# Attention's turns at every second row block of a projection, two actions in each

## The chip, the cores and the metric

The kernel runs on one core of a Trainium2 chip. A core has a matrix engine (PE, whose weight loads the profile lists apart as PEld), a vector engine (DVE), an activation engine (ACT), a general engine (POOL) and a queue that starts transfers (SP). The engines run side by side, each through its own list of instructions in order, and wait for one another by semaphores. The metric is the device time of one execution in microseconds (us).

## The reference

One layer of a hybrid decoder in float32, for 1024 rows of width 2048. The input is normalised by its rows' root mean square, multiplied by a matrix of 2048 x 6656, and the product is cut into two groups of heads:

- **stick-breaking** (16 heads of width 64): the weight of key s for query t is sigmoid(z) times the product of 1 - sigmoid(z) over the keys between them, over all earlier keys;
- **sliding window** (16 query heads on 4 key heads): a softmax over the last 128 keys, with a bias per distance and a learned extra logit per head.

Each group's result is normalised, gated with x * sigmoid(x) of a further slice of the projection, and both together go through an output matrix of 2048 x 2048. That is normalised again and added to the input.

## The kernel before

**Precision.** Each large product is made of three matrix products: both operands are split into a high part (a type that PE reads in one pass) and the rest, and high x high, high x rest and rest x high are summed in PSUM. So a weight chunk arrives by a transfer (L131), ACT makes its high part (L133), DVE the rest (L135).

**Projections.** The width 6656 is 52 column blocks of 128. The first three are done while the input arrives (to about 77 us). The other 49 follow one by one from the list `work`; `proj` runs each over four weight chunks (kg), two halves of 512 rows (h) and four blocks of 128 of the inner dimension (j): 4 x 2 x 4 = 32 steps of three matmuls 128x128 by 128x512. One such block of the inner dimension is a "row block" here. After each of the 32 steps `proj` calls `step()`. The 49 projections thus have 1568 steps.

**Attention between the steps.** Attention is cut into units, 160 for stick-breaking (8 pairs of heads, 20 units each; key `sb`) and 64 for the sliding window (4 groups, 16 units each; key `sw`). A unit has three actions on PE:

- *s1*: four score matmuls into a bank of tag "pz" (2 banks). ACT and DVE then turn scores into weights: two sigmoids, two scans and a product for `sb` (L530 to L546); bias, maximum, exponential, sum and scaling for `sw` (L614 to L629).
- *s2*: three or four 128x128 transposes of the weights into a bank of tag "pw" (2 banks), split by ACT (L561, L640) and DVE (L562, L641).
- *s3*: four matmuls with the values into the bank of tag "po" (only one bank). For `sw` each unit ends with a copy of this bank by ACT (L493) and a transfer; for `sb` one to four units share the accumulation before the copy.

A fourth kind, from the list `later`, holds deferred pieces, above all the two transposing pieces of a value block (`evac_v`, tile `vt`), which use "pw" too.

**Who comes next.** `advance()` runs at most one action. It looks, in this order, for a deferred piece that is due, an s3, an s2, an s1. "Due" goes by the planner's own clock `pe_time`, which adds up the nominal length of the matmuls written so far (0.64 for one step, 0.43 for a score or a value action, 0.33 or 0.44 for the transposes). An s2 is due 6.2 (`sb`) or 7.0 (`sw`) after its s1 was written, an s3 4.5 or 5.0 after its s2; s1 follow one another at 4.7 or 3.8, where the first two of a group may follow at once. At most three units stand between s1 and s2, at most three between s2 and s3. The order of PE's instructions is the order in which the program writes them; the other engines' lists are ordered by a scheduler under priorities.

**Deadlines.** When the values of pair p are projected, `drain` forces whatever is left of pair p - 1 (and, at the first, of the sliding window), without waiting for the due times. `background()` runs at each step as well and moves sums for the output product through POOL by the same clock.

**Output product.** From about 1504 us on, seven products of half size (a Strassen form) make the output, L907, with row scaling and residual at the end.

Of the kernel before, what the change touches and what calls it, by code (L numbers as in the profile page):

```python
# [57 lines left out]
def layer(ctx, tc, xT, x, w_first, w_blk, w_out, g_pre, g_post, g_sb, g_sw, sinks, rel, onehot, penalty, out):  # L58
# [93 lines left out]
    def advance(force=False):  # L152
        now = pe_time[0]
        while waiting and (force or waiting[0][0] <= now):
            todo.extend(waiting.pop(0)[1])
            prep()
        if later and (force or later[0][0] <= now):
            later.pop(0)[1]()
            return True
        if stage2 and (force or stage2[0][0] + stage2[0][1]["lag2"] <= now):  # L160
            u = stage2.pop(0)[1]
            u["s3"]()
            left[u["key"]] -= 1
            return True
        if stage1 and len(stage2) < 3 and (force or stage1[0][0] + stage1[0][1]["lag"] <= now):
            u = stage1.pop(0)[1]
            u["s2"]()
            stage2.append((pe_time[0], u))
            return True
        if todo and len(stage1) < todo[0]["depth"] and (force or last_start[0] + todo[0]["period"] <= now):  # L170
            u = todo.pop(0)
            if not u["ready"]:
                u["prep"]()
            last_start[0] = max(last_start[0] + u["period"], now - u["period"])
            u["s1"]()
            stage1.append((pe_time[0], u))
            prep()
            return True
        return False

    def prep():
        for u in todo[:AHEAD]:
            if not u["ready"]:
                u["ready"] = True
                u["prep"]()
# [4 lines left out]
    def background(force=False):  # L190
        for ch in chains:
            while force or pe_time[0] >= ch["at"]:
                if ch["job"] is None:
                    if not jobs:
                        break
                    ch["job"] = jobs.pop(0)(ch["buf"])
                wait = next(ch["job"], None)
                if wait is None:
                    ch["job"] = None
                else:  # L200
                    ch["at"] = pe_time[0] + wait
# [7 lines left out]
    def open_chain(buf, start):  # L209
        chains.append(dict(buf=buf.rearrange("p (a n) -> p a n", a=2), at=start, job=None))  # L210
# [38 lines left out]
    open_chain(row_sw, 112.0)  # L249
    open_chain(at.tile([P, 2 * HALF], F32, tag="bg", name="bg", bufs=1), 122.0)  # L250

    def step():
        advance()
        background()

    def drain(key):
# [195 lines left out]
    def proj(b, name, nxt=None, mid=None):  # L452
        def get(b, name, kg):
            return split_w(f"{name}_{kg}", w_blk[b, :, 4 * kg:4 * kg + 4, :])

        if not splits:
            splits.append(get(b, name, 0))
        ps = [pproj(f"p_{name}_{h}") for h in range(2)]
        for kg in range(4):
            wh, wl = splits.pop(0)  # L460
            if kg == 2 and mid is not None:
                mid()
            if kg < 3:
                splits.append(get(b, name, kg + 1))
            elif nxt is not None:
                splits.append(get(*nxt, 0))
            for h in range(2):
                for j in range(4):
                    k = 4 * kg + j
                    for i, (wt, xt) in enumerate(((wh, xh[k]), (wh, xl[k]), (wl, xh[k]))):  # L470
                        mm(ps[h], wt[:, j, :], xt[:, h * HALF:(h + 1) * HALF],
                           start=(k == 0 and i == 0), stop=(k == KT - 1 and i == 2))
                    step()
        return ps
# [535 lines left out]
```

## Time and profile before

| | us |
|---|---|
| median of 3 runs | 1807.02 |
| lowest and highest of the 3 | 1804.5 and 1808.76 |
| the profiled execution's own time | 1807.31 |
| its span from the first to the last instruction | 1805.6 |
| PE busy | 1780.6 (99%) |
| DVE busy | 1245.8 (69%) |
| ACT busy | 789.6 (44%) |
| POOL busy | 496.0 (27%) |

Busy time is the union of an engine's instructions. PE's matmuls overlap in the pipeline: a 128x512 matmul shows some 0.39 us, but the next starts about 0.23 us later. So distances between starts say what work costs on PE, and idle time before an instruction, with its releaser, says what a wait costs. The table of waits lists who waited for whom, the timeline lists instructions by start, and a table of windows gives the busy time in stretches of the span.

### The profile page before, as it was taken

How to read it: one execution, taken by the hardware profiler on the slowest of the kernel's cores; microseconds unless marked ns; L12 is line 12 of the kernel's file. 1: busy time of each engine (PE TensorE's matmuls, PEld its weight loads, DVE VectorE, ACT ScalarE, POOL GpSimd, SP SyncE). 2: the span in 40 equal slices, each digit the busy share in tenths (PEclk: the TensorE clock that was granted, in tenths of full speed). 3: DMA queues.
4: the chain of work that ended last, by engine and by line, in shares of the span. 5: the costliest groups of instructions: out<-in, count | busy, mean ns of one | idle time of the engine just before them, and what ended most of it. 6: DMA issues, size and time to landing. Idle time of an engine off the chain costs nothing. (4 is left out here: it accounts for less than half of the span.)

```text
span 1805.6 us, 27329 instructions
## 1 busy us (share of the span) xinstructions
PE 1780.6 (99%) x9046; PEld 1492.2 (83%) x9046; DVE 1245.8 (69%) x1984; ACT 789.6 (44%) x1696; POOL 496.0 (27%) x648
## 2 busy tenths in 40 slices
PE   8999999999999999999999999999999999999997
PEld 7788888888888888888888888888888887888886
DVE  7558852588567688587776787767858657746867
ACT  7335531355344444344443444434435434445433
POOL 0011121211213333133232322232313225504523
PEclk9999999999999999999999999999999999999999
DMA  7548675576747657466556564454435386634485
GB/s 230 193 138 219 199 223 148 167 210 206 224 124 199 182 164 195 142 182 184 175 163 185 153 183 129 137 169 139 151 91 140 98 258 210 198 105 129 143 250 184
DMA packets 203884, 312.48 MB, mean 173 GB/s; under 512 B 24640, under 2 KB 84192, under 8 KB 203616
## 3 DMA queue, kind: packets, MB, share of 16 engines
q1 hardware_dynamic: 201680, 307.60, 57.7%
q10 hardware_dynamic: 2064, 3.15, 0.5%
q8 instruction: 72, 1.18, 0.3%
q14 instruction: 68, 0.56, 0.1%
HBM read 219.42 MB, written 91.23 MB: 172 GB/s over the span
## 5 line engine op out<-in xcount | busy, mean ns | idle before, releaser
L543 DVE TENSOR_TENSOR_SCAN m_sb<-m_sb,m_sb,zero 128x257 f32<-128x257 f32 x192 | 157.3, 857 | 46.9 <-ACT m_sb L530 46.4
L530 ACT ACTIVATE m_sb<-z_sb 128x512 f32<-128x512 f32 x160 | 96.1, 601 | 132.1 <-PE z_sb L122 119.9
L546 DVE TENSOR_TENSOR b_sb<-b_sb,m_sb 128x512 f32<-128x512 f32 x160 | 129.0, 806 | 20.5 <-POOL b_sb L536 9.0
L540 DVE TENSOR_TENSOR_SCAN m_sb<-m_sb,mask 128x256 f32<-128x256 f32 x128 | 117.4, 953 | 35.2 <-ACT m_sb L530 34.5
L907 PE MATMUL y<-wohi,x 128*128 128x512 f32 x448 | 140.8, 390 | 0.0
L562 DVE TENSOR_TENSOR wl_sb<-wt_sb,wh_sb 128x512 fp32r<-128x512 f32 (+1 forms) x160 | 100.7, 631 | 57.7 <-ACT wh_sb L561 57.0
L561 ACT CAST wh_sb<-wt_sb 128x512 fp32r<-128x512 f32 (+1 forms) x160 | 86.9, 543 | 111.6 <-PE wt_sb L126 109.3
L907 PE MATMUL y<-wohl,x 128*128 128x512 f32 x576 | 132.8, 389 | 2.7 <-DVE wohl L773 2.7
L907 PEld LDWEIGHTS y<-wohl,x 128*128 128x128 f32 x576 | 108.0, 188 | 25.5 <-DVE wohl L773 3.1
L122 PE MATMUL p_qsb<-xh,whi_qsb 128*128 128x512 f32 x256 | 104.5, 408 | 0.0
L122 PE MATMUL p_ksb<-xh,whi_ksb 128*128 128x512 f32 x256 | 104.4, 408 | 0.0
L122 PE MATMUL p_zsw<-xh,whi_zsw 128*128 128x512 f32 x256 | 104.3, 407 | 0.0
L122 PE MATMUL p_vsb<-xh,whi_vsb 128*128 128x512 f32 x256 | 102.9, 402 | 0.0
L122 PE MATMUL p_zsb<-xh,whi_zsb 128*128 128x512 f32 x256 | 102.9, 402 | 0.0
L623 ACT ACTIVATE L_sw<-L_sw,nm_sw 128x256 f32<-128x256 f32 (+1 forms) x128 | 62.6, 490 | 91.6 <-DVE nm_sw L618 88.5
L122 PE MATMUL p_zsw<-xh,wlo_zsw 128*128 128x512 f32 x256 | 101.0, 394 | 0.0
L122 PE MATMUL p_ksb<-xh,wlo_ksb 128*128 128x512 f32 x256 | 100.9, 394 | 0.0
L122 PE MATMUL p_qsb<-xh,wlo_qsb 128*128 128x512 f32 x256 | 100.8, 394 | 0.0
L122 PE MATMUL p_ksb<-xl,whi_ksb 128*128 128x512 f32 x256 | 100.7, 394 | 0.0
L122 PE MATMUL p_zsw<-xl,whi_zsw 128*128 128x512 f32 x256 | 100.7, 393 | 0.0
L122 PE MATMUL p_vsb<-xh,wlo_vsb 128*128 128x512 f32 x256 | 100.7, 393 | 0.0
L122 PE MATMUL p_qsb<-xl,whi_qsb 128*128 128x512 f32 x256 | 100.6, 393 | 0.0
(242 smaller groups left out, 4974.3 us busy)
## 6 DMA issues: line engine op xcount, KB each, us to landing
row_sw<-in_w_out SPq DMA_DIRECT2D x80, 256.0 KB, 4.2
bg<-in_w_out SPq DMA_DIRECT2D x80, 256.0 KB, 4.5
woraw<-wsum SPq DMA_DIRECT2D x80, 256.0 KB, 3.3
kh<-kd SPq DMA_DIRECT2D x160, 64.0 KB, 3.3
kl<-kd SPq DMA_DIRECT2D x160, 64.0 KB, 3.1
wsum<-row_sw SPq DMA_DIRECT2D x40, 256.0 KB, 2.6
wsum<-bg SPq DMA_DIRECT2D x40, 256.0 KB, 3.1
q_sw<-qd SPq DMA_DIRECT2D x64, 128.0 KB, 3.6
```

The costliest lines, as they stand in the source:

```text
L122: tc.keep_in_program_order(nc.tensor.matmul(ps, a, b, start=start, stop=stop))
L530: nc.scalar.activation(m[:, :, 1:257], z, AF.Sigmoid, scale=-SCALE)
L540: nc.vector.tensor_tensor_scan(m[:, tb, 1:257], m[:, tb, 1:257], mask[:, P - P * tb:P - P * tb + 256], m[:, tb, 0:1], ALU.mult, ALU.max)
L543: nc.vector.tensor_tensor_scan(m[:, tb, :], m[:, tb, :], zero.to_broadcast([P, 257]), prev[:, tb, 256:257], ALU.mult, ALU.max)
L546: nc.vector.tensor_mul(beta, beta, m[:, :, 0:256])
L561: nc.scalar.copy(wh[:, :k], pt[:, :k])
L562: nc.vector.tensor_sub(wl[:, :k], pt[:, :k], wh[:, :k].bitcast(F32))
L623: nc.scalar.activation(L[:, hh, :n], L[:, hh, :n], AF.Exp, bias=nm[:, hh:hh + 1], accum_out=sm[:, hh:hh + 1])
L907: nc.tensor.matmul(ps, xt[:, a, tcols], w[b][:, cols], start=first and n == 0, stop=last and n == 2)
```

## The change

`step()` is called as often as before. `background()` still runs in each call. `advance()` now runs only in every second call, and there twice, so that up to two actions are written one behind the other with no projection step between them. Since a projection has 32 steps, the turns fall on the second and fourth row block of each chunk and half. Nothing else is edited: due times, limits, tiles and the matmuls themselves are the same.

```diff
+    turn = [0]
+
     def step():
-        advance()
+        turn[0] += 1
+        if turn[0] % 2 == 0:
+            advance()
+            advance()
         background()
```

## The prediction

> **What bounds the kernel now.** I read the page's table of engines first, then the time by stages, then PE's waits.
>
> ```profile
> span 1805.6 us, 27329 instructions
> ...
> PE 1780.6 (99%) x9046; PEld 1492.2 (83%) x9046; DVE 1245.8 (69%) x1984; ACT 789.6 (44%) x1696; POOL 496.0 (27%) x648
> ```
>
> The profiled execution took 1807.31 us, 1.7 around its span; the median of the three runs, 1807.02, is 0.3 below it. PE is busy in all but 25 us. The windows say where the 25 us lie (columns: stretch, its length, then busy time of PE, PEld, DVE, ACT, POOL, granted clock, DMA):
>
> ```profile
> 77.00:490.00 413.00, 407.89 (x2126) 341.07 (x2125) 267.83 (x673) 177.37 (x544) 79.69 (x63) 1.00 0.66 190
> 490.00:630.00 140.00, 140.00 (x735) 118.38 (x734) 89.21 (x126) 55.69 (x106) 36.95 (x64) 1.00 0.63 173
> 630.00:1440.00 810.00, 808.39 (x4329) 685.25 (x4328) 593.58 (x804) 359.44 (x681) 243.24 (x421) 1.00 0.53 154
> ...
> 1500.00:1806.00 306.00, 293.49 (x1309) 241.81 (x1307) 208.41 (x266) 127.08 (x257) 119.02 (x81) 0.99 0.54 172
> ```
>
> The edit acts between 77 and 1504 us. There PE idles 5.1 us in the sliding window's stretch (77 to 490) and 1.6 us in the stick-breaking stretches (490 to 1440). The 12.5 us after 1500 belong to the output product and the tail. PE's waits by name:
>
> ```profile
> PE f0a L122 <- ACT whi_f L308: 5.8, 1, 5.8
> PE y L907 <- DVE wohl L773: 2.7, 1, 2.7
> PE wt_sw L126 <- DVE L_sw L629: 2.4, 4, 1.1
> PE vt_vsw L126 <- DVE v_vsw L396: 1.9, 1, 1.9
> PE o_sb L122 <- DVE wl_sb L562: 1.6, 3, 0.9
> PE o_sw L122 <- ACT ot_sw L493: 0.7, 1, 0.7
> ```
>
> Attention's own waits are the last four, 2.4 + 1.9 + 1.6 + 0.7 = 6.6 us. That is the most that a better order of the same actions can give back in waits. The three bigger engines beside PE have spare time everywhere, so the time is PE's instructions plus its waits.
>
> **The change part by part.** *The number of actions.* 64 + 160 units of three actions and 20 deferred transposing pieces make 692 actions in 1568 steps. On the timeline no two of them stand together now; 373 times exactly one projection step lies between two, 168 times two. The new turns are 784, with room for 1568 actions, so the capacity is as before. Nothing is added to or taken from PE: the instruction count stays, and no DMA is added. What moves is (a) an action that is due at an odd step, one step later, (b) two actions that are due together, side by side, and (c) with each s1 its successors' operand loads, on SP's queue, by one step.
>
> *Side by side on PE.* The starts around the end of the first stick-breaking pair:
>
> ```profile
> 612.75 0.28 PE L122 MATMUL o_sb<-wl_sb,v_vsb 128*128 128x256 f32 x1
> 612.87 0.40 PE L122 MATMUL p_vsb<-xh,whi_vsb 128*128 128x512 f32 x1
> ...
> 613.57 0.49 PE L126 MATMUL wt_sb<-ident,b_sb 128*128 128x128 f32 x3
> ...
> 616.65 0.39 PE L122 MATMUL p_vsb<-xh,whi_vsb 128*128 128x512 f32 x1
> ...
> 618.69 0.39 PE L122 MATMUL p_vsb<-xh,whi_vsb 128*128 128x512 f32 x1
> ...
> 619.37 0.28 PE L122 MATMUL o_sb<-wh_sb,v_vsb 128*128 128x256 f32 x1
> ...
> 621.70 0.39 PE L122 MATMUL p_vsb<-xh,wlo_vsb 128*128 128x512 f32 x1
> ```
>
> A step between two actions takes 613.57 - 612.87 = 0.70 us. Far from any action three steps take 618.69 - 616.65 = 2.04, or 0.68 each. So the visit itself costs something: averaged over the timeline, the steps between two visits are 18 ns over that floor where one step lies between, 28 where two, 42 where four, 17.0 us in all. With turns two steps apart I count about 490 visits for the 692 actions: some 380 gaps at 28 ns and 110 at 42 make 15 us, **-2 us**. The bounds are 0 (the excess goes with the actions, not with the visits) and -4 (all actions in pairs, 346 gaps at 38).
>
> *The due times hold.* An s2 still waits its 6.2 or 7.0 after its s1. Its next turn after that is on average a step away instead of half a step, so operands are on average some 0.35 us more ready. For the sliding window I worked the clock through: in the steady state s1 come every four steps, and eight steps after an s1 the clock has 8 x 0.64 + 4 x 0.43 = 6.84 < 7.0, so its s2 comes at the tenth. Now 26 of 64 come at the eighth and 26 at the ninth. The 2.4 us on L_sw should mostly go: **-1.5** (bounds -2.4 and 0, the latter because DVE's chain is in order and may be late by as much). The 1.6 us on wl_sb: **-0.8** (-1.6 to +0.8). The one wait for ot_sw in the middle of a group: **-0.4** (-0.7 to 0).
>
> *Two outputs through one bank.* At the start of a group two s1 are written at once, already now. With pairs in a turn both s2 fall into one turn too, ten steps on, and by the clock both s3 into one, six steps after that. For `sw` both write the single "po" bank, with ACT's copy between them. The first such pair now:
>
> ```profile
> 127.07 0.28 PE L122 MATMUL o_sw<-wh_sw,v_vsw 128*128 128x256 f32 x1
> ...
> 127.54 0.39 PE L122 MATMUL p_qsw<-xh,whi_qsw 128*128 128x512 f32 x1
> ...
> 127.74 0.37 ACT L493 COPY ot_sw<-o_sw 128x256 f32<-128x256 f32 x1 [0.67 <-PE o_sw L122]
> ...
> 128.24 0.31 PE L122 MATMUL o_sw<-wh_sw,v_vsw 128*128 128x256 f32 x1
> ```
>
> The step at 127.54 hides the copy exactly: it is over at 128.11 and the second s3 starts at 128.24. Without that step the second could start at 127.54 and waits until about 128.2: a new wait of 0.65 us, more if ACT is in another instruction. Here ACT had idled 0.67 before; behind a 0.6 us cast it is 1.25. Four groups at 0.7: **+2.8** (bounds +2.6 and +5). Later in a group the s3 come two steps apart by my count and the copy is covered. For `sb` the pair accumulates in one bank with no copy between: 0. The pairs of s1 and s2 have two banks of their own.
>
> *Two value pieces.* The pieces of the first value block stand one step apart, with a wait behind it:
>
> ```profile
> 87.06 0.60 PE L126 MATMUL vt_vsw<-ident,u_vsw 128*128 128x128 f32 x4
> ...
> 89.64 0.42 DVE L396 TENSOR_TENSOR v_vsw<-vt_vsw,v_vsw 128x256 fp32r<-128x256 f32 x1
> 90.21 0.99 PE L126 MATMUL vt_vsw<-ident,u_vsw 128*128 128x128 f32 x4 [1.86 <-DVE v_vsw L396]
> ```
>
> The second waits for DVE's last read of the first. The lags are 9.0 and 10.0; the sixteenth step has 10.24, so both fall into one turn, the step between them goes behind both, and the wait grows by it: **+0.7**. The clock takes part here:
>
> ```profile
> 87.00:90.00 3.00, 1.36 (x8) 0.81 (x6) 2.07 (x4) 1.78 (x4) 0.58 (x1) 1.00 0.60 172
> 90.00:94.00 4.00, 3.79 (x12) 3.19 (x13) 1.52 (x4) 1.26 (x3) 1.96 (x2) 0.57 0.76 198
> ```
>
> After a stretch with PE busy 1.36 of 3 us the granted clock is 0.57 over the next 4 us, which costs 4 x 0.43 = 1.7 us and is in the time already. With a wait of 2.6 us I keep it: 0, bounds -1.7 and +1.7 (a second stretch like it).
> The Trainium skill ("TensorE: Matmul & The Clock Gate", "Why this matters for your kernels") lets the clock drop only at idle gaps beyond about 3 us; by that neither gap would cost clock, while this row shows a drop after 1.86 us, and the row decides.
>
> *Deadlines.* The last s3 of the pair stands at 619.37, and its value projection ends three steps later (621.70 is its last matmul). By the clock, the first s1 moves from step 9 to step 10 of its pair and the last s3 from 125 to 126 of 128: two steps of margin, nothing forced, **0**. If one s3 slipped a turn, it would be forced about six steps (4.2 us) after its s2, whose operands now take a median of 2.7 us: still about 0.
>
> *Weights, SP.* The rest part of a weight chunk is ready a median of 5.7 us before its first matmul, and PE has no wait on it above 0.2 us. One step (0.70) more or less in SP's order is covered. If that cover went at one chunk per projection, each step late would cost 0.70.
>
> The sum is -2 - 1.5 - 0.8 - 0.4 + 2.8 + 0.7 = -1.2, and 1807.3 - 1.2 = **1806.1 us**.
>
> **The rivals.** *Slower: the single output bank.* If the pairs of s3 don't come only at a group's start but recur, because s2 that are due at odd steps are rounded into the same turn, each pair costs 0.65 to 1.25 us on PE with nothing to cover it. Up to 32 pairs fit in 64 units: 21 to 40 us. It decides (over 3.6 us slower than before) from about eight pairs beyond my four; at twelve beyond, at 0.65, the sum is -1.2 + 7.8 = +6.6, or 1814. For it: only a step of 0.70 covers the copy now. Against it: the due times spread the s3 by four steps in the steady state, and the group is done 41 steps or more before it is needed.
>
> *Faster: the waits go.* The pairs find ACT free and the extra lag takes all the waits but the value piece's: -2.4 - 1.6 - 0.7 in waits, -4 in visits and +0.7 + 2.6 give -5.4, or 1802. For it: 0.35 us more readiness on average; against it: the 2.6 us of the bank pairs is arithmetic.
>
> *Forced actions.* The turns lag so far that each drain forces an s2 and its s3 back to back: eight drains at about 2.7 us (median from s2 to its split's end) are +22, or 1829. Against it: last s2 eleven steps, last s3 three steps before the end, and an equal capacity.
>
> **How the numbers follow.** What a measurement of this kernel tells from no change is about 0.2%, 3.6 us. Forecast (1806, no difference) 0.58; the bank 0.18 and forced actions 0.04, both slower; the waits go 0.20, faster. So faster 0.20, same 0.58, slower 0.22. The forecast's terms give 1800 with all low bounds at once (-4 - 2.4 - 1.6 - 0.7 + 2.6 + 0.7 - 1.7 = -7.1) and 1815.5 with all high ones (0.8 + 5 + 0.7 + 1.7 = +8.2); as they don't fall together, its own range is 1802 to 1811. Reaching to the other cases, the range is 1801 to 1813, which leaves out the forced case and half of the bank's.
>
> **What would show it right or wrong.** The count of PE's instructions the same; about 490 visits; waits on ot_sw by PE four times at 0.6 to 1.3 us, near the third turn after the first s2 of each `sw` group; the wait for L_sw near 1 us; vt_vsw at 2.6 us, and the clock still down after it; no two s3 of `sb` beyond a pair's end. It is wrong if PE waits for ot_sw ten times or more, if a projection's matmuls wait for weights, or if PE's starts grow by more than 0.1 us where two actions meet.

## The result, and the profile after

The changed kernel takes 1819.30 us (median of six runs, 1813.90 to 1823.34) against 1805.72 us for the kernel before (six runs, 1803.53 to 1808.76). The ratio is **1.0078, with a 95% interval of 1.0063 to 1.0094**. It is slower, by some 14 us, where the forecast was 1806 and no difference. The profiled execution took 1823.11 us, 15.8 more than the profiled one of before, and its trace is compared with that one below.

The page's head and table of engines after the change:

```profile
span 1821.4 us, 27339 instructions
...
PE 1781.3 (98%) x9046; PEld 1500.7 (82%) x9046; DVE 1255.3 (69%) x1984; ACT 793.7 (44%) x1696; POOL 499.8 (27%) x648
```

PE's instructions are as many as before and its busy time is 0.7 us more. So nearly all of the 15.8 us is idle time of PE. The windows (stretch, length, busy time of PE, PEld, DVE, ACT, POOL, granted clock, DMA share, GB/s):

```profile
77.00:490.00 413.00, 403.92 (x2122) 342.31 (x2121) 259.15 (x673) 180.04 (x543) 78.75 (x63) 1.00 0.66 190
490.00:630.00 140.00, 133.87 (x690) 113.27 (x689) 87.52 (x119) 53.29 (x100) 35.51 (x62) 0.98 0.58 159
630.00:1440.00 810.00, 804.37 (x4301) 684.42 (x4300) 607.61 (x799) 358.85 (x678) 247.15 (x418) 1.00 0.54 154
1500.00:1822.00 322.00, 308.01 (x1366) 253.59 (x1364) 214.63 (x277) 132.83 (x268) 121.32 (x84) 0.98 0.55 175
```

PE now idles 9.1 us in the first stretch (5.1 before), 6.1 in the second (0), 5.6 in the third (1.6) and 14.0 in the last (12.5). The names of its waits:

```profile
PE o_sb L122 <- DVE wl_sb L567: 8.3, 4, 5.3
...
PE o_sw L122 <- ACT ot_sw L498: 3.1, 4, 1.4
PE wt_sb L126 <- DVE b_sb L551: 2.7, 2, 1.9
PE wt_sw L126 <- DVE L_sw L634: 2.3, 6, 1.0
PE y L912 <- DVE wohl L778: 2.2, 1, 2.2
PE vt_vsw L126 <- DVE v_vsw L401: 2.2, 1, 2.2
PE y L912 <- ACT wohi L777: 1.7, 1, 1.7
PE z_sw L122 <- DMA q_sw<-qd: 1.5, 1, 1.5
PE p_qsb L122 <- DVE wlo_qsb L135: 0.6, 1, 0.6
```

The wait on wl_sb rose from 1.6 to 8.3 us and one on b_sb of 2.7 is new. Both are in the stick-breaking stretches, where the prediction had seen almost nothing to wait for.

The starts of the projections' 1568 steps on PE's timeline say where the two kernels part. At step 480, the end of the sliding window, the changed kernel is 0.5 us ahead (it was 1.2 ahead at the first step). It loses 8.3 us between steps 512 and 544, 1.7 between 576 and 608, 2.1 between 672 and 704 and 4.1 between 832 and 864. Elsewhere behind step 480 stretches of 32 steps differ by at most 0.7 us to either side. At the last step it is 14.1 us behind, and the output product adds 1.7.

**The largest place**, at 550 to 567 us. A gate of the sliding window there needs the stored attention output, `or_zsw`, which comes in two transfers on SP's queue. SP's timeline after:

```profile
550.56 0.60 SPq L414 DMA_DIRECT2D or_zsw<-od  x1
552.00 0.55 SPq L131 DMA_DIRECT2D wraw_zsw<-in_w_blk  x1
553.70 0.60 SPq L414 DMA_DIRECT2D or_zsw<-od  x1
```

and before:

```profile
548.60 1.66 SPq L409 DMA_DIRECT2D or_zsw<-od  x2
```

Before, both transfers were issued together. Now a weight load stands between them and the second is issued at 553.70. By the profile, SP's waits just before these two were ended by landings of background transfers: 0.8 us by a load of `bg` before the weight load, 1.1 us by a store of `row_sw` before the second `or_zsw`. Before, two such waits on loads of `bg` took 0.6 and 0.5 us here. The timeline of all engines after (start, us, engine; in brackets the idle time just before and what ended it):

```profile
560.81 1.28 POOL L416 TENSOR_TENSOR or_zsw<-or_zsw 128x512 f32<-128x512 f32 x1 [12.62 <-DMA or_zsw<-od]
...
562.08 0.62 POOL L541 TENSOR_SCALAR_AFFINE_SELECT b_sb<-b_sb 128x512 f32<-128x512 f32 x1
562.66 1.26 POOL L227 TENSOR_TENSOR bg<-bg 128x512 f32<-128x512 f32 x1
562.73 1.74 DVE L551 TENSOR_TENSOR b_sb<-b_sb,m_sb 128x512 f32<-128x512 f32 x1 [6.14 <-POOL b_sb L541]
...
564.18 1.42 POOL L227 TENSOR_TENSOR row_sw<-row_sw 128x512 f32<-128x512 f32 x1
564.40 1.74 DVE L135 TENSOR_TENSOR wlo_zsw<-wraw_zsw,whi_zsw 128x512 fp32r<-128x512 f32 x1
...
566.07 0.68 DVE L567 TENSOR_TENSOR wl_sb<-wt_sb,wh_sb 128x512 fp32r<-128x512 f32 x1
...
566.80 0.58 PE L122 MATMUL o_sb<-wl_sb,v_vsb 128*128 128x256 f32 x1 [5.28 <-DVE wl_sb L567]
```

It is a chain through three lists that are each in order. POOL stands 12.62 us at the sum of the two halves. Behind it in POOL's list is the masking of a diagonal unit (b_sb, L541), and DVE waits 6.14 us for that. Then two background sums (L227) run on POOL beside two products of DVE, which take 1.74 us each. Behind these two in DVE's list is wl_sb, and PE waits 5.28 us for it. The same place before:

```profile
556.07 1.45 POOL L411 TENSOR_TENSOR or_zsw<-or_zsw 128x512 f32<-128x512 f32 x1 [7.51 <-DMA or_zsw<-od]
...
557.51 0.62 POOL L536 TENSOR_SCALAR_AFFINE_SELECT b_sb<-b_sb 128x512 f32<-128x512 f32 x1
...
558.10 1.28 POOL L227 TENSOR_TENSOR bg<-bg 128x512 f32<-128x512 f32 x1
...
558.16 1.77 DVE L546 TENSOR_TENSOR b_sb<-b_sb,m_sb 128x512 f32<-128x512 f32 x1 [1.73 <-POOL b_sb L536]
```

The chain was there before, too: POOL stood 7.51 us, and DVE's product beside a background sum took 1.77 us. It ended just early enough that PE did not wait. The change did not make this chain; it made it longer than its cover.

### The profile page after: what moved, and what is told of

It reads as the page before. It is cut to its first block, busy times and chain, and to the rows that moved or that the text cites. A ratio compares the mean times of both kernels' runs of the same rounds, so it can differ in the third digit from the quotient of the medians.

```text
span 1821.4 us, 27339 instructions
## 1 busy us (share of the span) xinstructions
PE 1781.3 (98%) x9046; PEld 1500.7 (82%) x9046; DVE 1255.3 (69%) x1984; ACT 793.7 (44%) x1696; POOL 499.8 (27%) x648
## 4 chain that ended last, share of the span: by engine, by line
PE 73%; DVE 6%; DMA 6%; issue 1%; ACT 1%; POOL 1%; SPq 1%; DVEq 0%; ACTq 0%; POOLq 0%
PE y L912 12%; PE p_zsb L122 10%; PE p_ksb L122 9%; PE p_zsw L122 8%; PE p_vsb L122 8%; PE p_qsb L122 7%; PE p_qsw L122 4%; PE o_sb L122 4%; PE z_sb L122 4%; PE wt_sb L126 3%; DMA or_zsw<-od 2%; DMA xr<-in_x 1%; PE p_vsw L122 1%; DVE y L876 1%; PE o_sw L122 1%
## 5 line engine op out<-in xcount | busy, mean ns | idle before, releaser
L548 DVE TENSOR_TENSOR_SCAN m_sb<-m_sb,m_sb,zero 128x257 f32<-128x257 f32 x192 | 151.7, 828 | 42.4 <-ACT m_sb L535 42.0
L551 DVE TENSOR_TENSOR b_sb<-b_sb,m_sb 128x512 f32<-128x512 f32 x160 | 140.7, 879 | 27.5 <-POOL b_sb L541 13.4
L545 DVE TENSOR_TENSOR_SCAN m_sb<-m_sb,mask 128x256 f32<-128x256 f32 x128 | 113.7, 929 | 37.7 <-ACT m_sb L535 37.6
L912 PEld LDWEIGHTS y<-wohi,x 128*128 128x128 f32 x448 | 84.9, 190 | 20.0 <-ACT wohi L777 2.1
L122 PE MATMUL p_vsb<-xl,whi_vsb 128*128 128x512 f32 x256 | 100.7, 393 | 0.0
L541 POOL TENSOR_SCALAR_AFFINE_SELECT b_sb<-b_sb 128x512 f32<-128x512 f32 x64 | 49.1, 768 | 187.5 <-ACT b_sb L537 184.2
```

The lines of the kernel that those rows point to most:

```text
L122: tc.keep_in_program_order(nc.tensor.matmul(ps, a, b, start=start, stop=stop))
L541: nc.gpsimd.affine_select(out=beta, in_=beta, compare_op=ALU.is_gt, fill=0.0, base=0, pattern=[[-P, 2], [1, 256]], channel_multiplier=-1)
L545: nc.vector.tensor_tensor_scan(m[:, tb, 1:257], m[:, tb, 1:257], mask[:, P - P * tb:P - P * tb + 256], m[:, tb, 0:1], ALU.mult, ALU.max)
L548: nc.vector.tensor_tensor_scan(m[:, tb, :], m[:, tb, :], zero.to_broadcast([P, 257]), prev[:, tb, 256:257], ALU.mult, ALU.max)
L551: nc.vector.tensor_mul(beta, beta, m[:, :, 0:256])
L912: nc.tensor.matmul(ps, xt[:, a, tcols], w[b][:, cols], start=first and n == 0, stop=last and n == 2)
```

## The experiments

The loss stands where only background work, gates and stick-breaking meet, so four theories were set against one another. In the expectations they carry these letters. **A**: the gate's operand comes late, and POOL passes the lateness on. **B**: two actions in one turn crowd ACT and DVE by themselves. **C**: the lists of the other engines come out in another order, by chance, and any edit may do so. **D**, formed after the first two sets: it is the place of the background sums (`sum_job`: two loads, a POOL sum, a store) against attention and gates that counts.

The results first; "before" is the median of the kernel before in the same set of runs.

| kernel | median us | before | ratio (95%) |
|---|---|---|---|
| sw_pairs | 1815.23 | 1804.12 | 1.0063 (1.0042 to 1.0083) |
| sb_pairs | 1806.16 | 1804.12 | 1.0010 (0.9998 to 1.0022) |
| every | 1808.44 | 1804.12 | 1.0020 (1.0009 to 1.0032) |
| odd | 1810.76 | 1804.12 | 1.0036 (1.0020 to 1.0051) |
| after_apart | 1817.73 | 1805.16 | 1.0067 (1.0049 to 1.0085) |
| before_apart | 1810.25 | 1805.16 | 1.0027 (1.0014 to 1.0039) |
| after_hurry | 1826.20 | 1805.16 | 1.0121 (1.0099 to 1.0143) |
| after_again | 1816.56 | 1805.16 | 1.0072 (1.0048 to 1.0096) |
| after_bgbefore | 1811.55 | 1804.33 | 1.0043 (1.0028 to 1.0059) |
| before_bgafter | 1815.27 | 1804.33 | 1.0054 (1.0039 to 1.0070) |
| after_nosum | 1799.64 | 1804.33 | 0.9968 (0.9955 to 0.9981) |
| before_nosum | 1795.85 | 1804.33 | 0.9957 (0.9942 to 0.9972) |
| after_dmaonly | 1805.75 | 1804.17 | 1.0008 (0.9995 to 1.0021) |
| after_poolonly | 1812.83 | 1804.17 | 1.0054 (1.0035 to 1.0073) |
| before_poolonly | 1805.41 | 1804.91 | 1.0005 (0.9995 to 1.0015) |
| before_shift | 1810.98 | 1804.17 | 1.0048 (1.0032 to 1.0064) |
| before_paced | 1809.53 | 1804.17 | 1.0034 (1.0021 to 1.0047) |
| after_paced | 1812.18 | 1804.43 | 1.0043 (1.0027 to 1.0059) |

The five kernels with nosum, dmaonly or poolonly in their names leave out part of the background, so they don't compute the layer. None of the others is faster than the kernel before.

### The turns, in parts and in other rhythms

The first two kernels pair the turns in one half of the attention only.

```diff
 sw_pairs
-        if turn[0] % 2 == 0:
+        if turn[0] > 480:
+            advance()
+        elif turn[0] % 2 == 0:
 sb_pairs
-        if turn[0] % 2 == 0:
+        if turn[0] <= 480:
+            advance()
+        elif turn[0] % 2 == 0:
```

> Turns at every second step with two actions only for the first 480 steps (the sliding window); after that one action per step as before. Theory A (the time is lost in the stick-breaking stretch, where the load of attention's output for a gate, or_z, holds up POOL's list, and then DVE's and PE's): no loss, 1806 within 2. Theory B (two actions side by side crowd ACT and DVE wherever they stand): the loss of 13.6 us spreads over the actions, 192 of 692 of them here, so +3.8, about 1809.5.

> One action per step for the first 480 steps, paired turns only after that (stick-breaking). Theory A: the whole loss, 1817 to 1821. Theory B: 500 of 692 actions, +9.8, about 1815.5. A third theory C (the lists of the other engines come out in another order by chance, and nearly any shift of the planning costs some us): anywhere between 1806 and 1822, and with the longest waits at other gates than in the changed kernel.

The paired turns of the sliding window alone bring most of the loss, 1.0063, and those of stick-breaking alone bring none that can be told, 1.0010. Neither A (no loss, then the whole) nor B (1809.5, then 1815.5) expected that. And the loss of sw_pairs is not in the sliding window. Its profile loses 9.6 us after step 480, in the same kind of place (2.2 us in steps 512 to 544, 4.4 in 576 to 608, 5.6 in 832 to 864). From step 482 on its attention actions stand at the very steps where the kernel before has them. PE's waits of sw_pairs in the window from 505 to 1450 us:

```profile
PE wt_sb L126 <- DVE b_sb L553: 7.2, 3, 3.8
PE o_sb L122 <- DVE wl_sb L569: 0.9, 1, 0.9
```

Its largest wait, at 850 us in its timeline:

```profile
847.34 1.26 POOL L418 TENSOR_TENSOR or_zsw<-or_zsw 128x512 f32<-128x512 f32 x1 [7.27 <-DMA or_zsw<-od]
...
848.63 0.69 DVE L433 TENSOR_TENSOR u_zsw<-u_zsw,or_zsw 128x512 f32<-128x512 f32 x1 [6.27 <-POOL or_zsw L418]
...
849.24 0.68 DVE L553 TENSOR_TENSOR b_sb<-b_sb,m_sb 128x512 f32<-128x512 f32 x1
849.34 1.72 POOL L439 TENSOR_TENSOR acc_sw<-acc_sw,sg_zsw 128x512 f32<-128x512 f32 x1 [0.74 <-DVE u_zsw L433]
...
849.84 1.76 DVE L135 TENSOR_TENSOR wlo_vsb<-wraw_vsb,whi_vsb 128x512 fp32r<-128x512 f32 x1
...
850.07 0.63 PE L126 MATMUL wt_sb<-ident,b_sb 128*128 128x128 f32 x4 [3.83 <-DVE b_sb L553]
```

Here the gate's own product on DVE (u_zsw) waits 6.27 us for POOL's sum, the b_sb product stands behind it, and PE waits 3.83. B falls with this: a loss at places where attention stands as before isn't made by two actions standing together there. What does differ is the background. `background()` goes by `pe_time`, and two actions in one turn shift that clock at single steps, mostly by 0.2 to 0.9. Between steps 501 and 525 the background's pieces stand at steps 506, 509, 513, 516 and 523 before, at 502, 508, 509, 516, 518 and 524 in the changed kernel, and at 501, 507, 508, 515, 517, 522 and 525 in sw_pairs. Of the 83 pieces that the planner writes between steps 512 and 864 before, 7 have their old step in the changed kernel and none in sw_pairs. But such a move needn't cost anything: in sb_pairs only 6 have it, and no loss can be told.

Two other rhythms, two actions at any step and the odd turns in place of the even ones:

```diff
 every
-        if turn[0] % 2 == 0:
-            advance()
-            advance()
+        advance()
+        advance()
 odd
-        if turn[0] % 2 == 0:
+        if turn[0] % 2 == 1:
```

> Two chances at every step, so no action is rounded to a second step, and pairs stand together only where two are due at once. Theory A by rounding (late deferred pieces and late actions push the gate's load back): 1806 to 1809. Theory B (pairs): pairs are few here, 1806 to 1810. Theory C: anywhere between 1804 and 1822.

> The same change with the turns at the first and third row block instead of the second and fourth. Theory A and B: the same loss, 1815 to 1822, in A with the waits of POOL for or_z above 5 us again ahead of PE's longest waits. Theory C: a different sum, with the waits at other places.

The odd turns do nearly the same to attention as the even ones, a step apart (488 visits with an action in place of 471), and cost less than half as much (1.0036; the intervals do not meet). The rhythm as such isn't the price. PE's waits on wl_sb and b_sb in the window from 505 to 1450 us are 3.9 us in odd, 0.8 in every and 11.0 in the changed kernel.

### The gate

Theory A moved POOL's sum of the two halves from the place of the loads to the place of the gate, so that POOL's list does not stand at it so early:

```diff
     def load_o(name, tile_i, h):
...
+        return o2
+
+    def join_o(o2):
         nc.gpsimd.tensor_add(o2[:, 0, :], o2[:, 0, :], o2[:, 1, :])
         return o2[:, 0, :]
...
-        gate(0, early_o.pop(name))
+        gate(0, join_o(early_o.pop(name)))
         o1 = load_o(name, tile_i, 1)
         if last:
-            gate(1, o1)
+            gate(1, join_o(o1))
         else:
-            defer(6.0, lambda: gate(1, o1))
+            defer(9.0, lambda: gate(1, join_o(o1)))
```

> The changed kernel, with POOL's sum of the two parts of or_z taken away from the load and put at the gate itself (first half) or behind a lag of 9.0 instead of 6.0 (second half), so that POOL's list no longer stands at a transfer in flight. Theory A: the waits of POOL for or_z fall from 61.8 us to below 15 and the time comes back to 1805 to 1809. Theory B or C: 1815 to 1822 stays.

> The same move of POOL's sum in the kernel before, as the control. Theory A: before hides these waits almost wholly (1.6 us of PE's waits on wl_sb), so 1803 to 1807. Theory C: a shift like any other, 1806 to 1820.

> The changed kernel once more, for a second profile on this chip. If the long waits come from the order of the lists, they stand at the same steps again (near 561, 701, 714 and 852 us) within some tenths of a us; if from the transfer's chance, the lengths change by us from profile to profile. Time 1814 to 1823.

It does not help: 1.0067 beside 1.0072 for the changed kernel taken again, and the kernel before loses 0.27% by it. POOL waits for or_zsw 82.2 us in all in after_apart, 61.8 in the changed kernel and 48.6 before, so the edit lengthened that wait, and this pair doesn't test A. The changed kernel's second profile loses in the same stretches (7.1, 2.4, 1.5 and 2.4 us), so these places are the kernel's and not one execution's. The lengths vary by more than the tenths that were expected: its longest wait is 4.14 us in place of 5.28.

The other way is to put the two transfers ahead in SP's list:

```diff
+        with tc.high_priority(HURRY):
             for i in range(2):
                 nc.sync.dma_start(o2[i * HD:(i + 1) * HD], ...
```

> The changed kernel with the transfers of or_z at a higher priority in SP's list, so that no weight load stands between the two. Theory A with SP's order as the cause of the late landing: the 5.3 us wait near 561 us goes and about 5 to 8 us come back, 1811 to 1814. If the landing is late for the transfer itself (7 us under load), 1817 to 1821 stays.

This is the slowest kernel of all, 1.0121, with 14.8 us of waits on wl_sb and b_sb between 505 and 1450 us. At the largest place it did what A said. Both transfers are issued together at 545.88, and the loss between steps 512 and 544 falls from 8.3 to 2.1 us. But 4.4 us go between 576 and 608 (1.7 in the changed kernel), 4.9 between 832 and 864 (4.1), and some 2 each at two new places behind 960. So the late operand makes the longest wait, but A, in the form "bring the gate's operand sooner and the loss goes", falls. Both edits reorder SP's list, and the loss comes back at other places, as C would have it.

### The background sums

If D holds, the kernels must be alike without the sums. Without loads, POOL sum and store; the output product then reads one summand in place of the sum:

```diff
-            BG(nc.sync.dma_start(t[:, 0, :], w_view(a, e, cols)))
-            BG(nc.sync.dma_start(t[:, 1, :], w_view(b, e, cols)))
             yield 8.0
-            BG((nc.gpsimd.tensor_add if sign > 0 else nc.gpsimd.tensor_sub)(t[:, 0, :], t[:, 0, :], t[:, 1, :]))
             yield 6.0
-            BG(nc.sync.dma_start(wsum[i][e][:, cols], t[:, 0, :]))
             yield 6.0
...
-            nc.sync.dma_start(raw, wsum[i][e][:, cols] if i in wsum else w_view(PRODUCTS[i][0][0], e, cols))
+            nc.sync.dma_start(raw, w_view(PRODUCTS[i][0][0], e, cols))
```

> The changed kernel without the background sums of the output weights: no loads, no sums on POOL, no stores, and the output product reads one of the two summands instead (the five products that need a sum compute something else; the same number of matmuls). D: the waits of PE between steps 512 and 864 go, and the time is within 3 us of the kernel before under the same cut. If not D: 10 us or more above it.

> The same cut in the kernel before, as the control: 1800 to 1806, since PE waits little on attention here already.

The medians are 1799.64 and 1795.85, 3.8 us apart in place of 14, and the intervals of the two ratios overlap. In the profiles the two stand within 0.5 us of one another at the last projection step. (The profiled execution of before_nosum was its longest, 1802.05; the others took 1795 to 1797, and no trace shows where the 3.8 us of the medians lie.) PE's waits of after_nosum in the window from 505 to 1430 us:

```profile
PE o_sb L122 <- DVE wl_sb L563: 0.8, 2, 0.6
```

So the background sums are needed for most of the loss. The next pair asks for their place. A table of the clock that the background sees at each step, `BG_CLOCK`, was taken from one planner and used in the other kernel; attention keeps its own clock. In both traces PE's actions stand at the very steps at which they stood without this edit.

```diff
+    steps = [0]
+
+    def bg_now():
+        return BG_CLOCK[min(max(steps[0], 1), len(BG_CLOCK)) - 1]
+
     def background(force=False):
         for ch in chains:
-            while force or pe_time[0] >= ch["at"]:
+            while force or bg_now() >= ch["at"]:
...
-                    ch["at"] = pe_time[0] + wait
+                    ch["at"] = bg_now() + wait
```

> Theory D: the loss comes from the background sums. Their steps go by the planner's clock; the change shifts them against attention and the gates, and in four stretches (from steps 512, 576, 672 and 832) their transfers and POOL's sums fall ahead of what attention needs. sw_pairs, whose actions from step 480 on stand at the same steps as before, loses its 11 us there. This kernel has the paired turns, but the background pieces stand at the very steps of the kernel before. D: most of the loss goes, +0 to +4 us on the kernel before. If the pairs or the gates themselves cost the time: +10 to +14.

> The converse: attention's turns as before, one action per step, but the background pieces at the steps that they have in the changed kernel. D: most of the loss without the change, +8 to +13 us. If the pairs cost the time: within 3 us of the kernel before.

The clearest of all is the second. With the attention of before, and nothing but the background at the steps of after, the kernel loses 0.54% (0.39 to 0.70). PE's waits of before_bgafter from 505 to 1450 us, where the kernel before has its 1.6 us on wl_sb alone:

```profile
PE wt_sb L129 <- DVE b_sb L555: 4.2, 3, 3.2
PE o_sb L125 <- DVE wl_sb L571: 3.7, 5, 2.1
```

The converse gives back only a part: 1.0043 in place of 1.0078 (the intervals do not meet). That is 7 us on the kernel before, between the two ranges that were expected. The same window still shows 0.5 us on b_sb and

```profile
PE o_sb L125 <- DVE wl_sb L576: 4.1, 2, 2.1
```

So it isn't that the background's old steps are good by themselves. The two together speak for how they lie against attention; the order of the other engines' lists, which comes out anew in both (C), is not separated from that. The smallest shift that leaves all else alone starts the two chains three units of the clock later, in the kernel before:

```diff
-    open_chain(row_sw, 112.0)
-    open_chain(at.tile([P, 2 * HALF], F32, tag="bg", name="bg", bufs=1), 122.0)
+    open_chain(row_sw, 115.0)
+    open_chain(at.tile([P, 2 * HALF], F32, tag="bg", name="bg", bufs=1), 125.0)
```

> The kernel before with nothing moved but the start of the two background chains, 115 and 125 of the planner's clock instead of 112 and 122. If where the background stands decides: a change of some us, 1 to 12 slower, in the stretch from step 512 to 864. If not: within 2 us of the kernel before.

That alone costs 0.48% (0.32 to 0.64). Its profiled execution was the shortest of its six, 1807.64 against the median of 1810.98. Even so, its trace loses 5.6 us between steps 672 and 704, in the stretch that was named, with 2.8 us of waits on b_sb and 2.0 on wl_sb. The old arrangement of attention and background was a favourable one, and it is easily lost.

PE's waits above 0.3 us stand at few places. In the traces of this section and the two before it most are near steps 542, 590, 686 to 698, 814 and 846, whatever was edited. An edit decides which of these wait, and how long.

### Which half of a sum

Transfers without POOL's sum, and POOL's sums without transfers (on tiles that are filled once at the start; the product reads one summand):

```diff
 after_dmaonly
-            BG((nc.gpsimd.tensor_add if sign > 0 else nc.gpsimd.tensor_sub)(t[:, 0, :], t[:, 0, :], t[:, 1, :]))
 after_poolonly, before_poolonly
-            BG(nc.sync.dma_start(t[:, 0, :], w_view(a, e, cols)))
-            BG(nc.sync.dma_start(t[:, 1, :], w_view(b, e, cols)))
...
-            BG(nc.sync.dma_start(wsum[i][e][:, cols], t[:, 0, :]))
...
+    bg = at.tile([P, 2 * HALF], F32, tag="bg", name="bg", bufs=1)
+    nc.gpsimd.memset(row_sw, 1.0)
+    nc.gpsimd.memset(bg, 1.0)
```

> The changed kernel with the background's loads and stores but without its sums on POOL (what is stored is the first summand alone, so the five products that need a sum compute something else). If the transfers do it: the loss stays, 10 us or more above the kernel before. If POOL does it: about 1796 to 1803, as without any background work.

> The changed kernel with the background's sums on POOL, on tiles filled once, but without its loads and stores (the output product reads one summand, so five products compute something else). If POOL does it: the loss stays, 1810 or more. If the transfers do it: about 1796 to 1803. If it takes both, in that a late landing and a sum ahead of the next select add up, both this and the run without sums lie at 1796 to 1805.

> The kernel before with the background's sums on POOL on tiles filled once, without its loads and stores (five products of the output compute something else). If the sums on POOL alone make the difference between the two turn rules: 1797 to 1803, 10 us or more below after_poolonly (1812.8). If the sums on POOL cost both kernels alike: 1809 to 1814, within 4 us of it.

With POOL's sums alone the changed order still costs 0.49% (1.0054 less 1.0005, intervals apart), though before_poolonly lies in neither of its expected ranges. But it costs it elsewhere: the two part by about 8 us before step 480, where the pairs of the sliding window stand, so B isn't excluded there. Between 77 and 487 us PE idles 11.0 us in after_poolonly and 5.1 in before_poolonly, from there to 1440 us 2.5 and 2.4. PE's waits over the whole run of after_poolonly:

```profile
PE wt_sw L126 <- DVE L_sw L634: 5.9, 6, 2.0
...
PE o_sw L122 <- ACT ot_sw L498: 2.9, 6, 0.8
```

and of before_poolonly, where no wait on ot_sw is listed:

```profile
PE wt_sw L126 <- DVE L_sw L629: 3.0, 7, 0.5
```

With transfers alone the changed kernel takes 1.0008, 0.40% or some 7 us over the one without sums, with 5.4 us lost between steps 832 and 864. Its partner in the old order was not run, so what the transfers alone make of the difference stays open. In the full kernel the late landing and POOL's sums meet at the same gates, and their shares are not separated.

### Two versions that pace the background

Both hold the background back between 500 and 760 of the clock, where most of the loss was, and let it catch up later:

```diff
+                    if jobs or ch["buf"] is not None:
+                        wait *= 0.5 if not (todo or stage1 or stage2) else 0.7 if pe_time[0] > 760.0 else 1.0
                     ch["at"] = pe_time[0] + wait
+                    if 500.0 < ch["at"] < 760.0:
+                        ch["at"] = 760.0 + (5.0 if ch is chains[-1] else 0.0)
```

> The kernel before with the background halted between 500 and 760 of the planner's clock (about steps 540 to 840), its waits halved where no attention is under way, and at 0.7 behind 760. If the background in that stretch is what can cost time: 1800 to 1804, since before loses only 2 to 3 us there; slower if the denser background later starts to cost.

> The changed kernel with the same pacing of the background as before_paced. If the background against attention is the cause: within 3 us of before_paced, some 10 us faster than the changed kernel. If something else in the paired turns costs the time: 1815 or more.

1.0034 and 1.0043: the changed order improves from 1.0078 and the old one gets worse. The two are within 3 us, as expected if the background against attention is the cause. A gap in the background that is made by hand is not better than the old arrangement. Denser sums are not what costs it: between steps 864 and 1088 before_paced has 75 pieces where the kernel before has 53, and its trace loses 0.8 us there. The loss stands at two places, 3.7 us between steps 512 and 544, where the halt begins, and 4.0 between 1120 and 1152, behind the dense stretch, each with one long wait on b_sb (1.86 and 2.38 us).

## Why the prediction was wrong

**The visits: right.** The timeline has 471 visits, 250 with one action and 221 with two (about 490 were predicted), and the excess of the steps between them over the floor fell from 17.0 to 14.1 us: -2.9, where -2 was said.

**Deadlines: right, exactly.** The last s3 stands at step 126 of 128 in seven of the eight pairs and at 124 in the other, and no action is forced.

**Two outputs through one bank: right in sum, half by its mechanism.** The wait on ot_sw is 3.1 us in four places, 2.4 more than before, and the two terms on it gave +2.4. The timeline shows a pair of s3 in one turn:

```profile
124.85 0.28 PE L122 MATMUL o_sw<-wl_sw,v_vsw 128*128 128x256 f32 x1
125.59 0.39 PE L122 MATMUL o_sw<-wh_sw,v_vsw 128*128 128x256 f32 x1 [0.46 <-ACT ot_sw L498]
```

The second starts 0.74 us after the last matmul of the first, where 0.12 is usual: 0.62, beside the 0.65 worked out. But only two of the four groups have such a pair. The other two waits, 0.79 and 1.4 us, are single s3 that find ACT's copy late. That the sum agrees is in part luck. The rival of the many bank pairs did not come.

**Two value pieces.** The wait is 2.2 us, +0.3 where +0.7 was said. The clock gave 1.7 us back, the low bound: it stayed at 1.00 after this wait (the windows below). That is luck of one execution, since the changed kernel's second profile has 0.57 here.

**The wait on L_sw: wrong in its mechanism.** 2.3 us in place of 2.4, where -1.5 was said. From a unit's scores to its transposes lie 8.81 steps on average in place of 8.78: the units are written hardly later than before, so there was little readiness to gain. The prediction put the steady s2 at the tenth step; 40 of the 64 come at the eighth, 22 at the tenth and 2 at the twelfth. The second profile shows 1.2 us, so the size isn't settled by one execution.

**The operand loads: named, not priced.** "With each s1 its successors' operand loads, on SP's queue, by one step" stood in the list of what moves. The sum had no term for it; a wait of 1.5 us on q_sw is new (0.4 in the second profile).

**The step that failed** is "The 1.6 us on wl_sb: -0.8 (-1.6 to +0.8)", and under it two sentences: "operands are on average some 0.35 us more ready", and "The three bigger engines beside PE have spare time everywhere, so the time is PE's instructions plus its waits". The wait on wl_sb went up by 6.7 us and the one on b_sb by 2.7, against a bound of +0.8; the second profile has +5.2 and +3.2. The readiness did not come: in stick-breaking an s3 stands 6.18 steps after its s2 on average, before and after, and an s2 8.39 steps after its s1 in place of 8.58. And the bound priced readiness by the due times of attention alone. It left out that other work stands ahead in the same lists: DVE was idle for 6.14 us just before the late product, behind a POOL that was itself idle for 12.62. Spare time of an engine covers nothing when its list stands at one instruction. And the front part says that the background goes "by the same clock": its pieces moved too, yet they were no part of the change in the prediction. Its list of what moves, (a), (b) and (c), lacked a (d), the background. The kernel before with (d) alone loses 0.54%.

None of the rivals had this mechanism. Its chances for "slower" went to the bank and to forced actions, and neither came.

**The clock.** Two of the new waits are followed by a stretch at a lower clock. The windows of the changed kernel:

```profile
87.00:90.00 3.00, 0.83 (x7) 0.72 (x7) 2.03 (x5) 1.56 (x5) 0.45 (x1) 1.00 0.42 134
90.00:94.00 4.00, 4.00 (x19) 3.29 (x18) 1.37 (x3) 1.19 (x3) 2.13 (x2) 1.00 0.88 297
561.00:567.00 6.00, 0.72 (x4) 0.39 (x3) 4.27 (x4) 0.19 (x1) 5.62 (x11) 0.85 0.17 43
568.00:572.00 4.00, 4.00 (x14) 3.41 (x13) 3.58 (x6) 1.39 (x4) 1.68 (x2) 0.50 0.79 238
852.00:855.00 3.00, 1.11 (x7) 0.88 (x7) 2.35 (x3) 2.35 (x6) 2.26 (x2) 1.00 0.24 88
855.00:859.00 4.00, 4.00 (x14) 3.29 (x13) 3.90 (x5) 1.01 (x2) 4.00 (x5) 0.57 0.64 193
```

4 us at 0.50 and 4 at 0.57 cost 4 x 0.50 + 4 x 0.43 = 3.7 us. In the changed kernel's second profile the last stretch has 1.00 and the first has this:

```profile
87.00:90.00 3.00, 1.42 (x9) 0.97 (x7) 1.52 (x3) 1.36 (x3) 0.00 (x0) 1.00 0.63 172
90.00:94.00 4.00, 3.42 (x11) 2.92 (x12) 1.89 (x5) 1.88 (x4) 2.10 (x2) 0.57 0.68 209
```

So a term of this size comes and goes with the execution.

**The sum as measured**: visits -2.9, L_sw -0.1, ot_sw +2.4, vt +0.3, clock -1.7 and +3.7, q_sw +1.5, wl_sb +6.7, b_sb +2.7, wlo_qsb +0.6, and the output product's waits +1.2 (1.7 on wohi new, wohl 2.7 to 2.2). Together +14.4, beside the 15.8 of the two profiled executions. The prediction's own terms without the one on wl_sb gave -0.4 and measured -2.9 - 0.1 + 2.4 + 0.3 - 1.7 = -2.0, or -0.3 without the clock's chance. As a sum those were near enough; the term on wl_sb and the ones that had no place in the sum made the result.

**What stays open.** Why an arrangement is bad at just these places is shown for two chains only, at 560 us in the changed kernel and at 850 us in sw_pairs. The shares of late landing and POOL's sums are not separated. The swap of the background's clock gives back 0.35 of the 0.78%, so the background's steps alone are not the whole cause either; that the rest is their place against attention and gates is argued. That the lists of SP, POOL and DVE are reordered by the scheduler at every such edit takes part in all these kernels, and no run held all lists fixed.

## What to carry to other kernels

When work is planned by a clock, list everything that reads this clock: an edit that seems to move one kind of work moves all of them against one another. An engine at 27% or 69% busy still sets the time if its list is in order and one instruction in it waits for a transfer; so ask, for each operand with little cover, what stands ahead of it in its engine's list, and not how busy that engine is. Where a small shift of background work alone changes the time by 0.5%, as here, a forecast of a reordering should carry that much to either side, mostly the slower side when the order before shows almost no waits. And one trace doesn't size a term of 1 us: two of the same kernel differed by that much on L_sw, q_sw and the clock.

## What the runs showed of the hardware

**A DVE product beside a POOL operation ends just after it.** DVE's 128x512 products take 0.69 us alone (median of the 160 b_sb products before: 692 ns, longest 1780). In the rows above, four of them start 0.06 to 0.50 us after a POOL operation on two tiles has started. POOL's ended at 563.92, 565.60, 559.38 and 851.06 us, DVE's at 564.47, 566.14, 559.93 and 851.60: 0.54 or 0.55 us later each time. That fits a DVE product that stands until POOL's is over, but 1.19 to 1.22 us of POOL's operation were left at each of DVE's starts, so these rows alone can't tell it from a fixed delay. The rest of the changed kernel's trace can:

```profile
660.16 1.30 POOL L437 TENSOR_TENSOR acc_sw<-acc_sw,sg_zsw 128x512 f32<-128x512 f32 x1 [1.01 <-ACT sg_zsw L436]
...
660.54 0.68 DVE L371 TENSOR_TENSOR u_zsw<-p_zsw,rstd 128x512 f32<-128x512 f32 x1
...
661.14 0.87 DVE L431 TENSOR_TENSOR u_zsw<-u_zsw,or_zsw 128x512 f32<-128x512 f32 x1
```

The second DVE product starts with only 0.32 us of POOL's operation left, and it too ends 0.55 after it. The trace has 80 DVE products of b_sb, wlo and u_z with both inputs in SBUF that start while POOL works on two tiles. 75 of them end 0.53 to 0.57 us after POOL's operation, with 0.16 to 2.34 us of it left at their start; the other 5 start with at most 0.10 left and take 0.67 to 0.69. So it is no fixed delay. The first DVE product above, one input of which is the projection's sum in PSUM, isn't held. The Trainium skill ("SBUF — State Buffer", "SBUF: two separate sides") states such a rule: an operation of DVE with two SBUF inputs and one of GpSimd that reads SBUF exclude one another, and whichever starts first holds the shared port pair for the whole instruction. This trace agrees with it. It made a background sum on POOL cost 1.05 to 1.08 us in DVE's list in the rows above.

**The drop of the granted clock does not follow the length of one wait.** It was 0.57 after PE had been busy 1.36 of 3 us before the change, and 1.00 at the same place after 0.83 of 3 us; 0.50 after 0.72 of 6 us; 0.57 after 1.11 of 3 us with a longest wait of 1.89. The changed kernel itself gave 1.00 in one profile and 0.57 in the other behind the same wait of 2.17 us. Of six other kernels with the wait of 1.9 us of the kernel before, five show 1.00 behind it and one 0.59. No run here shows what else decides.
